# Three small tiles move to the constants pool, and TensorE's operand tiles start at byte 480 of 512

## The chip, the cores and the metric

The kernel runs on one core of one Trainium2 chip. The metric is device time in microseconds (us), as the median of timed runs of the whole program. One execution was also recorded by the hardware profiler; all traces below are such recordings.

## What is computed

One layer of a streaming encoder: 512 positions of width 1,024, everything in float32. Cut to what carries the time:

```python
mod = silu(c) @ w_ada + b_ada                       # 6 vectors of 1,024
xn  = rmsnorm(h, norm1_g) * (1 + sc1) + sh1
p   = xn @ w_in                                     # 512 x 1,024 by 1,024 x 8,200
q,k = silu(causal_dwconv(p[q|k columns]))
y_a = gmlp(p[u], p[v])                              # 128 x 128 mixing per channel group
y_b = mlstm(q, k, p[mv], p[o], p[i], p[f])          # 4 heads of 256, causal
h   = h + g1 * ((sigmoid(p[ga]) * y_a + sigmoid(p[gb]) * y_b) @ w_out)
xn  = rmsnorm(h, norm2_g) * (1 + sc2) + sh2
h   = h + g2 * (relu(xn @ w_ff1) ** 2 @ w_ff2)      # FFN width 4,096
out = rmsnorm(h, final_g)
```

## The kernel before

**Matmuls.** Nearly all the time goes to large matmuls. Each float32 operand is split into a rounded part (`h`) and the rest (`l`), both of TensorE's rounded float32 type, and a product is three matmuls into the same PSUM bank, `mm3` at lines 107 to 109: high by high, high by low, low by high. A matmul takes a stationary operand of 128 columns (`lhsT`, loaded into the array by a weight load of its own) and a moving operand of 512 or 256 columns (`rhs`). In the names of the profile, `out<-moving,stationary`.

**Stages**, in order of time:

1. The start: `x` is transposed, the modulation vectors are summed, and 6 banks of q and k are made in 8 chunks (`mm_w`, line 273): moving `xh`/`xl`, stationary `wh_s`/`wl_s`; 18 matmuls of 512 columns in a chunk.
2. The rest of `w_in`. Twelve "token-major" blocks (`block_tm`: o0, mv0, mv1, gb0, o1, gb1, v0, v1, u0, u1, ga0, ga1) have the weights as moving operand (512 columns) and a 128-column slice of `xh`/`xl` as stationary one; a block is 96 matmuls. Three "feature-major" blocks (`block_fm`: k1, q1 with 96 matmuls, k2 with 48) have it the other way round. Between them stand the scores and the attention products of the mLSTM, and the mixing of the gMLP.
3. The output projection `wo`: moving weights, stationary slices of `mhl`; 192 matmuls of 512 columns.
4. FF1: the first 512 columns (`f10b`, 192 matmuls of 256 columns), then 7 blocks of 7 products (`P`, Strassen-like, 24 matmuls of 256 columns each, 1,176 in all): moving `x2h`, `x2l`, `S..hl`, stationary `wh_B`, `wh_T` and their low parts.
5. FF2 (`ob`): 32 pieces of `w_ff2` of 128 rows, each 24 matmuls of 512 columns, with the weights moving and slices of `hsh`/`hsl` stationary. The first two pieces take their stationary operand from `sc` (`hs` in the names); the last four (`LAST`) have buffers of their own for the weights (`lwh`, `lwl` in `hsp`) and are run token block by token block, with the final norm behind each.

**Feeding.** The DMA queue brings a raw piece into `raws`, ScalarE rounds it (`act.copy`), VectorE subtracts (`dve.tensor_sub`), and the pair lies in `wpool`, three deep, prefetched two ahead (`Stream`). The order of the instructions on an engine is that of the program as built; nothing is decided at run time.

**Where tiles lie.** A pool is a stretch of bytes, the same on all 128 partitions. Pools of the left side are laid one behind the other from the bottom up, those with `side="right"` from the top down, and in a pool each tile starts at the next multiple of 32 bytes. So a small tile shifts every left tile behind it. In `before`, `const` ends at byte 18,816 (36 x 512 + 384), and `raws` and `wpool` follow there. `xpool` holds `yb` (16,384 bytes) and `hs` (64 bytes), which puts `xnp` at byte 448 of 512; `ffp` begins with `ss2` and `rs2` (32 bytes each with their padding), which puts its ring `hT` at byte 0 of 512. Slices of 128, 256, 512 or 1,024 elements step by whole multiples of 512 bytes, so every slice of a tile has its tile's offset. Only `vh` and `vl` (rows of 258 elements) vary.

| tiles | operand of | start, byte of 512 |
|---|---|---|
| `raw_*` (raws) | DMA target | 384 |
| `wh_*`, `wl_*` (wpool) | moving or stationary weights | 384 |
| `xh`, `xl` (xnp) | stationary or moving activations | 448 |
| `q..h`, `k..h` and low parts (attn) | scores | 448 |
| `wo3h` to `wo7l`, `f10..h`, `f10..l`, `h`, two of the eight `x2` pairs (ring `hT`) | wo, f10b | 0 |
| `sc`, `T` (ffp) | first two FF2 pieces | 0 |
| `mhl`, `S..hl` (mhp, right) | wo, P | 480 |
| the other `x2h`, `x2l` (x2p, right) | P, f10b | 480 |
| `hsh`, `hsl`, and `wh_f`, `wl_f` of the last four pieces (hsp, right) | FF2 | 480 |
| `wh_s`, `wl_s` of k at the start (stp, right) | start | 480 |
| `wgs` (right), `ones_r` | gates, row sums | 384, 256 |

Of the kernel before, what the change touches and what calls it, by code (L numbers as in the profile page):

```python
# [8 lines left out]
F32 = mybir.dt.float32  # L9
# [7 lines left out]
P = 128  # L17
# [3 lines left out]
TB = T // P  # L21
H = 4
# [18 lines left out]
V_GI = 144  # L41
V_GF = 145
NV = 146


@with_exitstack
def block_kernel(ctx, tc, vecs_d, rows_d, ws_d, x_d, w_ada, w_in, w_out, w_ff1, w_ff2, out_d):
# [3 lines left out]
    const = ctx.enter_context(tc.tile_pool(name="const", bufs=1))  # L51
# [6 lines left out]

    vecs = const.tile([P, NV], F32, name="vecs")
    ident = const.tile([P, P], F32, name="ident")  # L60
# [10 lines left out]
    def rsq(o, i):  # L71
        pool.tensor_scalar(out=o, in0=i, scalar1=EPS, scalar2=None, op0=ALU.add)
        pool.tensor_tensor(out=o, in0=o, in1=mhalf[:, 0:o.shape[-1]], op=ALU.pow)

    a2 = const.tile([P, KT], F32, name="a2")
    b2 = const.tile([P, KT], F32, name="b2")

# [32 lines left out]

    xpool = ctx.enter_context(tc.tile_pool(name="xpool", bufs=1))
    yb = xpool.tile([P, TB, D], F32, name="yb")
    hs = xpool.tile([P, TB, H], F32, name="hs")

    win = ExitStack()
    xnp = win.enter_context(tc.tile_pool(name="xnp", bufs=1))
# [525 lines left out]
    def ada_acc(base, nm):  # L642
        acc = pp.tile([P, D], F32, tag="acc", name="acc" + nm, bufs=2)

        def piece(k):
            raw = pp.tile([P, D], F32, tag="araw", name=f"ar{nm}{k}", bufs=3)
            sp.dma_start(out=raw, in_=w_ada[k * P:(k + 1) * P, base:base + D])
            if k == 0:
                dve.tensor_scalar(out=acc, in0=raw, scalar1=c_act[:, 0:1], scalar2=None, op0=ALU.mult)
            else:  # L650
                dve.scalar_tensor_tensor(out=acc, in0=raw, scalar=c_act[:, k:k + 1], in1=acc,  # L651
                                         op0=ALU.mult, op1=ALU.add)

        bg.extend([(lambda k=k: piece(k)) for k in range(KT)])
        return acc
# [109 lines left out]
    fp = ff.enter_context(tc.tile_pool(name="ffp", bufs=1))  # L765
    xr = yb
    for t in range(TB):
        sp.dma_start(out=xr[:, t, :], in_=x_d[t * P:(t + 1) * P, :])
    ss2 = fp.tile([P, TB], F32, name="ss2")
    rs2 = fp.tile([P, TB], F32, name="rs2")  # L770
    acc_g2 = ada_acc(5 * D, "g2")

    def pair_banks(nm, pr):
# [373 lines left out]
```

## Time and profile before

| | us |
|---|---|
| median of 3 timed runs | 836.16 |
| their range | 835.72 to 840.86 |
| span of the profiled execution, first to last instruction | 834.4 |
| median less span (what lies around it) | 1.8 |
| TensorE (PE) busy | 822.7 (99%) |
| VectorE (DVE), ScalarE (ACT) busy | 553.4 (66%), 359.5 (43%) |
| DMA, share of 16 engines | 39.6% |

The profile's page gives the busy time of each engine and, in 40 slices of the span, its busy share in tenths. Matmuls are pipelined: the recorded duration of one (389 to 400 ns for 512 columns) is longer than the time from its start to the next one's start. So the rate is read from starts. The view of one tile's instructions gives, for a group, the count, the least, median and greatest duration, and the first and the last start. Where the three lines of `mm3` run in turn, three steps lie between two starts of one line. The view by windows gives the number of matmuls in a stretch of time.

### The profile page before, as it was taken

The numbers are of one execution on the slowest core, as the hardware profiler recorded it, in microseconds if no ns is written. First come the engines' busy times: TensorE is split into PE (matmuls) and PEld (weight loads), VectorE is DVE, ScalarE is ACT, GpSimd is POOL, SyncE is SP. The second block draws the span as 40 slices with busy tenths as digits, with TensorE's granted clock in tenths as the row PEclk, the third lists the DMA queues.
The fourth block names the chain that finished last, engine by engine and source line by source line (L and its number), as shares of the span: only waits on it lengthen the run. The fifth ranks groups of instructions, "written<-read, shape, count | busy, mean of one in ns | idle before, by whom it ended". The sixth has DMA issues, their size and how long they took to land.

```text
span 834.4 us, 11373 instructions
## 1 busy us (share of the span) xinstructions
PE 822.7 (99%) x4427; PEld 700.2 (84%) x4427; DVE 553.4 (66%) x857; ACT 359.5 (43%) x540; POOL 42.2 (5%) x60
## 2 busy tenths in 40 slices
PE   8999999999999999999999999999999999999996
PEld 6887888887888888888888899999999888888885
DVE  5979657584733377888566689888888434443546
ACT  5557456274333233222444456666666221221314
POOL 2003020130100000100000000000000000000000
PEclk9999999999999999999999999999999999999998
DMA  9973331143033398676344231333321422222302
GB/s 274 269 239 107 105 97 26 43 135 101 3 98 101 114 340 290 211 266 218 106 179 144 84 122 49 105 108 114 106 77 65 138 101 101 78 99 101 111 15 102
DMA packets 66822, 107.28 MB, mean 129 GB/s; under 512 B 5328, under 2 KB 38224, under 8 KB 66768
## 3 DMA queue, kind: packets, MB, share of 16 engines
q1 hardware_dynamic: 66768, 106.56, 39.6%
q8 instruction: 35, 0.57, 0.3%
q14 instruction: 19, 0.16, 0.1%
HBM read 104.44 MB, written 2.10 MB: 128 GB/s over the span
## 4 chain that ended last, share of the span: by engine, by line
PE 94%; ACT 1%; DMA 1%; issue 1%; DVE 1%; POOL 0%; SPq 0%; POOLq 0%; DVEq 0%
PE ob L108 7%; PE ob L109 7%; PE ob L107 7%; PE P L107 6%; PE P L108 6%; PE P L109 6%; PE qk L273 4%; PE wo L107 1%; PE wo L108 1%; PE wo L109 1%; PE cp L232 1%; PE k1b L107 1%; PE u1b L107 1%; PE mv1b L109 1%; PE gb0b L108 1%
## 5 line engine op out<-in xcount | busy, mean ns | idle before, releaser
L107 PE MATMUL ob<-wh_f,hsh 128*128 128x512 f32 x240 | 94.9, 395 | 0.0
L108 PE MATMUL ob<-wl_f,hsh 128*128 128x512 f32 x240 | 94.9, 395 | 0.0
L109 PE MATMUL ob<-wh_f,hsl 128*128 128x512 f32 x240 | 94.9, 395 | 0.0
L85 ACT CAST wh_f<-raw_f 128x1024 fp32r<-128x1024 f32 x28 | 29.5, 1053 | 115.2 <-PE ob L109 112.1
L86 DVE TENSOR_TENSOR wl_f<-raw_f,wh_f 128x1024 fp32r<-128x1024 f32 x28 | 34.3, 1225 | 58.2 <-ACT wh_f L85 57.1
L107 PEld LDWEIGHTS ob<-wh_f,hsh 128*128 128x128 f32 x240 | 45.2, 188 | 10.8
L108 PEld LDWEIGHTS ob<-wl_f,hsh 128*128 128x128 f32 x240 | 45.2, 188 | 10.8
L109 PEld LDWEIGHTS ob<-wh_f,hsl 128*128 128x128 f32 x240 | 45.2, 188 | 10.8
L908 ACT CAST wh_T<-T 128x1024 fp32r<-128x1024 f32 x21 | 22.0, 1049 | 24.3 <-PE P L108 23.4
L107 PE MATMUL P<-x2h,wh_B 128*128 128x256 f32 x112 | 31.7, 283 | 0.0
L108 PE MATMUL P<-x2l,wh_B 128*128 128x256 f32 x112 | 31.6, 282 | 0.0
L109 PE MATMUL P<-x2h,wl_B 128*128 128x256 f32 x112 | 31.4, 280 | 0.0
L908 ACT CAST wh_B<-B 128x1024 fp32r<-128x1024 f32 x21 | 22.1, 1051 | 18.1 <-PE P L108 16.7
L1027 DVE CAST hsh<-h 128x512 fp32r<-128x512 f32 x30 | 12.7, 426 | 25.6 <-PE ob L108 25.6
L909 DVE TENSOR_TENSOR wl_T<-T,wh_T 128x1024 fp32r<-128x1024 f32 x21 | 25.7, 1225 | 2.9 <-ACT wh_T L908 2.9
L909 DVE TENSOR_TENSOR wl_B<-B,wh_B 128x1024 fp32r<-128x1024 f32 x21 | 25.6, 1221 | 0.5 <-ACT wh_B L908 0.5
L86 DVE TENSOR_TENSOR wl_gb<-raw_gb,wh_gb 128x1024 fp32r<-128x1024 f32 x8 | 9.8, 1224 | 20.7 <-ACT wh_gb L85 20.7
L1028 DVE TENSOR_TENSOR hsl<-h,hsh 128x512 fp32r<-128x512 f32 x30 | 20.7, 691 | 3.0 <-DVE hsh L1027 0.5
L651 DVE SCALAR_TENSOR_TENSOR accg<-arg,c_act,accg 128x1024 f32<-128x1024 f32 x14 | 17.9, 1282 | 5.2 <-DMA arg<-in_w_ada 5.0
L109 PEld LDWEIGHTS P<-x2h,wl_B 128*128 128x128 f32 x112 | 21.3, 190 | 0.0
L108 PEld LDWEIGHTS P<-x2l,wh_B 128*128 128x128 f32 x112 | 21.0, 188 | 0.0
L107 PEld LDWEIGHTS P<-x2h,wh_B 128*128 128x128 f32 x112 | 20.9, 187 | 0.0
(544 smaller groups left out, 2492.3 us busy)
## 6 DMA issues: line engine op xcount, KB each, us to landing
raw_f<-in_w_ff SPq DMA_DIRECT2D x36, 512.0 KB, 3.3
B<-in_w_ff SPq DMA_DIRECT2D x28, 512.0 KB, 3.8
ar<-in_w_ada SPq DMA_DIRECT2D x64, 128.0 KB, 3.4
arg<-in_w_ada SPq DMA_DIRECT2D x16, 512.0 KB, 5.6
raw_o<-in_w_in SPq DMA_DIRECT2D x8, 512.0 KB, 3.7
raw_mv<-in_w_in SPq DMA_DIRECT2D x8, 512.0 KB, 3.5
raw_gb<-in_w_in SPq DMA_DIRECT2D x8, 512.0 KB, 3.6
raw_v<-in_w_in SPq DMA_DIRECT2D x8, 512.0 KB, 3.5
```

The lines of the kernel that those rows point to most:

```text
L85: act.copy(out=wh, in_=raw)
L86: dve.tensor_sub(out=wl, in0=raw, in1=wh.bitcast(F32))
L107: pe.matmul(out, lhsT=ah, rhs=bh, start=start, stop=False)
L108: pe.matmul(out, lhsT=ah, rhs=bl, start=False, stop=False)
L109: pe.matmul(out, lhsT=al, rhs=bh, start=False, stop=stop)
L232: pe.matmul(cps[c][:, o:o + 1], lhsT=tile_[:, vi, f * P:(f + 1) * P], rhs=rhs, start=first and q == 0, stop=last and q == len(todo) - 1)
L273: pe.matmul(bk, lhsT=wx[:, kk, f * P:(f + 1) * P], rhs=xx[k], start=k == 0 and ps_ == 0, stop=k == KT - 1 and ps_ == 2)
L651: dve.scalar_tensor_tensor(out=acc, in0=raw, scalar=c_act[:, k:k + 1], in1=acc, op0=ALU.mult, op1=ALU.add)
L908: act.copy(out=wh, in_=src)
L909: dve.tensor_sub(out=wl, in0=src, in1=wh.bitcast(F32))
L1027: dve.tensor_copy(out=h_, in_=src)
L1028: dve.tensor_sub(out=l_, in0=src, in1=h_.bitcast(F32))
```

## The change

`hs`, `ss2` and `rs2` become tiles of the constants pool, and an unused tile of 480 bytes follows them there. `const` grows by 64 + 32 + 32 + 480 = 608 bytes and ends at byte 19,424 (37 x 512 + 480). `xpool` then holds `yb` alone, and `ffp` begins with its ring.

```diff
@@ -41,6 +41,7 @@
 NV = 146
+ROW_PAD = 480
@@ -72,6 +73,10 @@
+    hs = const.tile([P, TB, H], F32, name="hs")
+    ss2 = const.tile([P, TB], F32, name="ss2")
+    rs2 = const.tile([P, TB], F32, name="rs2")
+    const.tile([P, ROW_PAD // 4], F32, name="row_pad")
     a2 = const.tile([P, KT], F32, name="a2")
     b2 = const.tile([P, KT], F32, name="b2")
@@ -110,7 +115,6 @@
     yb = xpool.tile([P, TB, D], F32, name="yb")
-    hs = xpool.tile([P, TB, H], F32, name="hs")
@@ -766,8 +770,6 @@
         sp.dma_start(out=xr[:, t, :], in_=x_d[t * P:(t + 1) * P, :])
-    ss2 = fp.tile([P, TB], F32, name="ss2")
-    rs2 = fp.tile([P, TB], F32, name="rs2")
     acc_g2 = ada_acc(5 * D, "g2")
```

All the tiles of the table above then start at byte 480, but for `wgs` and `ones_r`, which stay. `vh`, `vl` and `ph` of the attention move from 160, 224 and 288 to 192, 256 and 320; their distances change little. Pools of the right side do not move.

No engine's instructions change in kind, number or order. Only two waits differ, both on GpSimd (POOL), because `ss2` and `rs2` no longer take bytes that other tiles used before. In the order of GpSimd before, from the first of the second norm's four pairs to the end:

```order
L72 TENSOR_SCALAR rs_3767<-ss_3766 128x1 [waits DMAHW0_49,PE_49,DMAHW1_49,Activation_49,Pool_49]
L73 TENSOR_TENSOR rs_3767<-rs_3767,mhalf 128x1 [waits Pool_49]
L72 TENSOR_SCALAR rs_3767<-ss_3766 128x1 [waits Activation_49]
...
L73 TENSOR_TENSOR rs_3767<-rs_3767,mhalf 128x1 [waits Pool_49]
L1090 TENSOR_TENSOR rs_7227<-rs_7227,mhalf 128x1 [waits DVE_49] x4
```

The same place in the changed kernel:

```order
L73 TENSOR_SCALAR rs_83<-ss_82 128x1 [waits Activation_49]
L74 TENSOR_TENSOR rs_83<-rs_83,mhalf 128x1 [waits Pool_49]
L73 TENSOR_SCALAR rs_83<-ss_82 128x1 [waits Activation_49]
...
L1092 TENSOR_TENSOR rs_7228<-rs_7228,mhalf 128x1 [waits DMAHW0_49,DMAHW1_49,DVE_49,PE_49]
L1092 TENSOR_TENSOR rs_7228<-rs_7228,mhalf 128x1 [waits DVE_49] x3
```

The first pair of the second norm (`rs2`) waits for ScalarE alone now; the first of the last norm (`rs3`), whose bytes now overlap older tiles, waits for two DMA queues and TensorE as well.

## The prediction

> **What bounds the kernel now.** The page first: busy times, TensorE's row of slices and its clock, and the chain that ended last.
>
> ```profile
> PE 822.7 (99%) x4427; PEld 700.2 (84%) x4427; DVE 553.4 (66%) x857; ACT 359.5 (43%) x540; POOL 42.2 (5%) x60
> PE   8999999999999999999999999999999999999996
> PEclk9999999999999999999999999999999999999998
> PE 94%; ACT 1%; DMA 1%; issue 1%; DVE 1%; POOL 0%; SPq 0%; POOLq 0%; DVEq 0%
> ```
>
> TensorE is busy in every slice at full clock and is 94% of the chain. The view of waits, for TensorE alone, says how little it stands still:
>
> ```profile
> PE xt L312 <- POOL epsc L298: 2.5, 1, 2.5
> PE xt L306 <- DVE xt L324: 1.6, 2, 1.3
> PE k1b L107 <- ACT wh_k L85: 0.2, 1, 0.2
> ```
>
> These are 4.3 us of 834.4, and 4.1 of them lie in the first 11 us. No faster transfer or split can help; the end moves only with the step of the matmuls, the time from one start to the next. A busy share doesn't show that step, so I read it from first and last starts, by stage. FF2's loop and its last four pieces, in the view of the tile `ob` (count, duration in ns least/median/greatest, first and last start):
>
> ```profile
> L107 PE MATMUL ob<-wh_f,hsh x200: 392/397/400, 659.6 to 799.5; 128*128 128x512 f32 x100
> L107 PE MATMUL ob<-wh_f,hsh x31: 389/389/389, 805.8 to 826.2; 128*128 128x512 f32 x31
> ```
>
> In the loop 199 x 3 steps take 139.9 us: 234.3 ns each. In the last pieces 30 x 3 steps take 20.4 us: 226.7 ns, and all 31 durations are the same to the nanosecond. It is the same matmul with the same kind of stationary operand (`hsh`, byte 480); the moving operand lies at 384 in the loop and at 480 in the last pieces. The other stages of 512 columns:
>
> ```profile
> L107 PE MATMUL mv1b<-wh_mv,xh x32: 394/394/394, 179.6 to 201.3; 128*128 128x512 f32 x32
> L107 PE MATMUL u0b<-wh_u,xh x32: 393/396/398, 331.4 to 353.1; 128*128 128x512 f32 x32
> L107 PE MATMUL k2b<-xh,wh_k x16: 392/392/392, 168.6 to 178.9; 128*128 128x512 f32 x16
> L108 PE MATMUL k2b<-xl,wh_k x16: 394/394/394, 168.8 to 179.1; 128*128 128x512 f32 x16
> L109 PE MATMUL k2b<-xh,wl_k x16: 388/388/389, 169.1 to 179.3; 128*128 128x512 f32 x16
> L107 PE MATMUL ob<-wh_f,hs x16: 390/393/404, 647.8 to 658.2; 128*128 128x512 f32 x16
> L107 PE MATMUL wo<-wh_wo,mhl x24: 391/398/476, 431.3 to 474.0; 128*128 128x512 f32 x24
> L107 PE MATMUL wo<-wo4h,mhl x8: 393/395/397, 444.0 to 476.8; 128*128 128x512 f32 x8
> L273 PE MATMUL qk<-xh,wh_s x42: 388/392/503, 21.7 to 56.9; 128*128 128x512 f32 x42
> ```
>
> Token-major blocks (moving 384, stationary 448): 21.7 us / 93 = 233.3 ns, in `mv1b` and in `u0b`. Feature-major (448, 384): 10.3 / 45 = 228.9. First FF2 pieces (384, 0): 10.4 / 45 = 231.1. `wo` is broken by other work, so I go by its median durations: a duration is 162 to 163 above its step (397 and 234.3; 389 and 226.7), so 398 and 395 (moving 384 and 0, stationary 480) make about 235 and 232.5. The start's 392 makes 229.5. So each pair of offsets has a step of its own, and the last pieces have the shortest. Their durations repeat without any spread, as if two periodic things stood at a fixed distance; that is my reading of it.
>
> **Does it need equal offsets, or the quiet end of the program?** FF1's first block answers. In its second half the first two pairs have both operands at byte 0, the others 480 against 0, with the same work around them:
>
> ```profile
> L107 PE MATMUL f10b<-x2h,f100h x8: 280/283/283, 495.1 to 497.6; 128*128 128x256 f32 x8
> L108 PE MATMUL f10b<-x2l,f100h x8: 283/283/283, 495.2 to 497.7; 128*128 128x256 f32 x8
> L108 PE MATMUL f10b<-x2l,f104h x8: 277/280/285, 501.1 to 503.6; 128*128 128x256 f32 x8
> 495.18 0.28 PE L108 MATMUL f10b<-x2l,f100h 128*128 128x256 f32 x1
> 497.70 0.28 PE L108 MATMUL f10b<-x2l,f100h 128*128 128x256 f32 x1
> 500.98 0.28 PE L107 MATMUL f10b<-x2h,f104h 128*128 128x256 f32 x1
> 506.30 0.28 PE L107 MATMUL f10b<-x2h,f106h 128*128 128x256 f32 x1
> ```
>
> Equal: all at 283 after the first, 21 steps in 2.52 us, 120.0 ns. Unequal: spread from 277 to 285, 45 steps in 5.32 us, 118.2 ns. So the fixed step comes with equal offsets in the middle of the program too, and at 256 columns it is no gain. The products, unequal now (480, 384), stand at 120.0: the view by windows, for the tile `P` (start:end, length, busy time and count of TensorE):
>
> ```profile
> 540.00:600.00 60.00, 60.00 (x502) 60.00 (x501) 13.94 (x21) 1.74 (x3) 1.00 0.35 106
> ```
>
> A matmul lasts some 0.28 us, so two or three of the 502 began before the window; 500 in 60.00 us is 120.0 ns.
>
> **The change part by part.** All pairs become 480 and 480. I take 226.7 ns for 512 columns and 120.0 ns for 256:
>
> - token-major, 12 x 96 = 1,152 matmuls: (233.3 - 226.7) = 6.6 ns each, 7.6 us
> - FF2, 28 pieces of 24 in the loop: 26 x 24 = 624 x 7.6 = 4.7 us, and the first two, 48 x 4.4 = 0.2 us; the last 96 gain nothing
> - `wo`, 72 x 8.3 + 120 x 5.8 = 1.3 us
> - feature-major, 240 x 2.2 = 0.5 us
> - the start, 144 x 2.8 = 0.4 us
>
> Together 14.7 us over 2,400 matmuls. Against it: `f10b`, 144 of its 192 go from 118.2 to 120.0, 0.3 us; and finding the fixed step again after a break, where the row of `f100h` shows one odd matmul (280 before 283). At 30 breaks, an estimate, of 10 ns (three odd matmuls of about 3 ns) that is 0.3 us. The 1,176 products: nothing, from 120.0 to 120.0. Their bounds: 116.1 (the gain of 512 columns in proportion, 226.7 / 234.3) and 123 (a duration of 286, the longest of the low rows, less 163): 4.6 us less to 3.5 us more. I take the row of `f100h`, the same shape with equal offsets. Scores, attention products, transposes, gates and row sums: too few, or their distance stays; nothing.
>
> What the moved bytes do elsewhere. Splits and casts on the two kinds of offset that are there already:
>
> ```profile
> L85 ACT CAST wh_f<-raw_f 128x1024 fp32r<-128x1024 f32 x28 | 29.5, 1053 | 115.2 <-PE ob L109 112.1 <-PE P L108 3.1
> L1051 ACT CAST wh_f<-raw_f 128x1024 fp32r<-128x1024 f32 x4 | 4.2, 1046 | 4.5 <-DMA raw_f<-in_w_ff 4.5
> L86 DVE TENSOR_TENSOR wl_f<-raw_f,wh_f 128x1024 fp32r<-128x1024 f32 x28 | 34.3, 1225 | 58.2 <-ACT wh_f L85 57.1
> L1052 DVE TENSOR_TENSOR wl_f<-raw_f,wh_f 128x1024 fp32r<-128x1024 f32 x4 | 4.9, 1220 | 2.0 <-ACT wh_f L1051 2.0
> B<-in_w_ff SPq DMA_DIRECT2D x28, 512.0 KB, 3.8
> raw_f<-in_w_ff SPq DMA_DIRECT2D x36, 512.0 KB, 3.3
> ```
>
> Writing to 480 (the rows of four) takes what writing to 384 takes, 1,046 and 1,053 ns, 1,220 and 1,225 ns. Half of the 28 transfers `B` land at 480, half at 384, and their common 3.8 us is far within the lead: ScalarE waits 112 us in the FF2 loop for TensorE to free a buffer. A piece will take 24 x 226.7 = 5.4 us there instead of 5.6; the split needs 1.05 and 1.23 us of it. So the cover stays. Where it is thin I bound the loss: the 0.2 us wait of `k1b` can grow by what `o0b` gains, 96 x 6.6 = 0.6 us; `wo`'s 1.3 and the start's 0.4 can be lost if splits and loads don't come earlier. Padding costs no instruction. GpSimd's changed waits: `rs2` loses waits for things long past, and the first `rs3` gains them behind a wait for VectorE that lasts to the end anyway; only four small powers and the last output are queued behind it, and TensorE's work is over. Nothing either way.
>
> The sum: 14.7 - 0.3 - 0.3 = 14.1 us, span 834.4 - 14.1 = 820.3, and with the 1.8 us that lie around the span 822.1, some 1.7% below the median of 836.16.
>
> [...]
>
> **The rivals.**
>
> [...] 7%.
>
> *The products gain too*, at 116.1: 4.6 us more, 817.5. Against it, the row of `f100h`. 6%.
>
> *The gain is given back at thin places.* Up to 0.6 + 1.3 + 0.4 us from above, and a slower return to the fixed step: six steps lost at each of 30 breaks, 30 x 6 x 6.6 ns = 1.2 us. Together 3.5: 825.6. For it, the waits of `k1b`, and the fact that the scores, below, never settled. 9%.
>
> *Slower: equal offsets collide.* The scores have both operands at 448 now. Their second head, durations by group:
>
> ```profile
> L108 PE MATMUL sc<-q2l,k2h 128*128 128x512 f32 x1 | 0.4, 402 | 0.0
> L109 PE MATMUL sc<-q2h,k2l 128*128 128x512 f32 x1 | 0.4, 396 | 0.0
> L107 PE MATMUL sc<-q3h,k3h 128*128 128x512 f32 x1 | 0.4, 397 | 0.0
> L109 PE MATMUL sc<-q3h,k3l 128*128 128x512 f32 x1 | 0.4, 387 | 0.0
> ```
>
> Equal, yet not settled within six matmuls, and one at 402, a step of 239. If the long runs settled there, the 1,152 would lose 5.7 ns, the 672 of the loop about 4.9, `wo` about 5.6, the other 384 about 9.9: 6.6 + 3.3 + 1.1 + 3.8 = 14.8 us, 851. It decides from a step of 232.9 on, the mean of the 2,400 now. Against it, the last pieces settled at 389 within three matmuls. 3%.
>
> That the tiles don't lie where the change says is excluded: the sizes in front of them add up to 480. The remaining 75% is the forecast.
>
> **How the numbers follow.** The forecast itself spreads from 820 to 824 (steps known to 0.5 ns over 2,400 matmuls). The range takes in the gain of the products below and the thin places above, with half of the distance to no effect: 817 to 828. Outside lie no effect, slower, and a little else, about 12%. A measurement of this kernel tells 1% (8.4 us) from no change: faster by that is below 827.8, which holds for the forecast, the products and the thin places, 0.89; within 1% for no effect and a half gain, 0.08; slower 0.03.
>
> **What would show it.** In the changed profile `ob`'s and the token-major rows should read 389/389/389, with 93 steps of a block in 21.1 us instead of 21.7; `k2b`'s three lines should become alike; `P` should keep 500 matmuls in 60 us, at 283 without spread. TensorE's waits should stay under 6 us. I am wrong if the token-major rows keep a spread around 394, if `P` leaves 120, or if new waits of TensorE for `wh_` tiles appear.

## The result, and the profile after

The changed kernel took 824.24 us (median of 4 runs, 822.58 to 824.85), the kernel before 836.45 us (median of 4, 835.72 to 840.86). The ratio is 0.9837, with a 95% interval of 0.9805 to 0.987. A second measurement of the same two kernels (below) gave 0.9837 again, 0.9818 to 0.9856. The profiled execution of the changed kernel took 822.58 us, the lowest of its four runs; its span is 820.8 us, against 834.4 before.

The page of the changed kernel: busy times, TensorE's slices and its clock, and the chain that ended last.

```profile
PE 809.9 (99%) x4427; PEld 702.0 (86%) x4427; DVE 553.2 (67%) x857; ACT 359.5 (44%) x540; POOL 42.1 (5%) x60
PE   8999999999999999999999999999999999999996
PEclk9999999999999999999999999999999999999999
PE 97%; DVE 1%; issue 1%; ACT 1%; DMA 0%; POOL 0%; POOLq 0%
```

TensorE's busy time fell by 12.8 us, VectorE's and ScalarE's stayed. TensorE is still busy in every slice and carries more of the chain, 97% instead of 94%. The view of its waits:

```profile
PE xt L316 <- POOL epsc L302: 2.5, 1, 2.5
PE xt L310 <- DVE xt L328: 0.7, 1, 0.7
PE k1b L112 <- ACT wh_k L90: 0.2, 1, 0.2
```

The same three waits, 3.4 us instead of 4.3, and no new one; the whole difference lies in `xt`, in the start. The matmuls by tile (count, duration in ns least/median/greatest, first and last start; the lines of `mm3` are 112 to 114 now): FF2 with its first two pieces in the second row, two token-major blocks, the feature-major one, `wo`, and the products.

```profile
L112 PE MATMUL ob<-wh_f,hsh x240: 388/389/390, 650.1 to 812.6; 128*128 128x512 f32 x120
L112 PE MATMUL ob<-wh_f,hs x16: 389/389/397, 639.2 to 649.4; 128*128 128x512 f32 x16
L112 PE MATMUL mv1b<-wh_mv,xh x32: 388/389/390, 178.3 to 199.4; 128*128 128x512 f32 x32
L112 PE MATMUL u0b<-wh_u,xh x32: 389/389/390, 326.4 to 347.5; 128*128 128x512 f32 x32
L112 PE MATMUL k2b<-xh,wh_k x16: 389/389/390, 167.5 to 177.7; 128*128 128x512 f32 x16
L113 PE MATMUL k2b<-xl,wh_k x16: 389/389/390, 167.7 to 177.9; 128*128 128x512 f32 x16
L114 PE MATMUL k2b<-xh,wl_k x16: 389/389/390, 167.9 to 178.1; 128*128 128x512 f32 x16
L112 PE MATMUL wo<-wh_wo,mhl x24: 389/390/476, 423.9 to 465.7; 128*128 128x512 f32 x24
L112 PE MATMUL P<-x2h,wh_B x112: 282/283/284, 498.1 to 627.3; 128*128 128x256 f32 x112
```

What stood at 394 and 397 stands at 389, with 1 ns of jitter; 93 steps of a token-major block take 21.1 us, as `u0b` shows; the three lines of `k2b` are alike; `P` stays at 283. Over all uninterrupted pairs of starts in `ob` the mean step is 226.7 ns.

Where the 13.6 us between the two spans came from, by the first start of each stage's first tile in the two traces (us; the forecast is the term of the sum):

| from, to | before | after | gain | forecast |
|---|---|---|---|---|
| span's start to `o0b` | 58.01 | 58.39 | -0.38 | 0.4 |
| `o0b` to `wo` (12 token-major and 3 feature-major blocks, attention, mixing) | 373.28 | 365.55 | 7.7 | 8.1 |
| `wo` to `f10b` | 50.36 | 49.24 | 1.1 | 1.3 |
| `f10b` to `P` | 24.99 | 24.91 | 0.1 | -0.3 |
| `P` to `ob` | 141.11 | 141.12 | 0.0 | 0 |
| `ob` to the span's end | 186.59 | 181.59 | 5.0 | 4.9 |

### The profile page after: what moved, and what is told of

Its sections match the earlier page's. It is cut to its first block, busy times and chain, and to the rows that moved or that the text cites. A ratio compares the mean times of both kernels' runs of the same rounds, so it can differ in the third digit from the quotient of the medians.

```text
span 820.8 us, 11373 instructions
## 1 busy us (share of the span) xinstructions
PE 809.9 (99%) x4427; PEld 702.0 (86%) x4427; DVE 553.2 (67%) x857; ACT 359.5 (44%) x540; POOL 42.1 (5%) x60
## 4 chain that ended last, share of the span: by engine, by line
PE 97%; DVE 1%; issue 1%; ACT 1%; DMA 0%; POOL 0%; POOLq 0%
PE ob L112 7%; PE ob L114 7%; PE ob L113 7%; PE P L114 6%; PE P L113 6%; PE P L112 6%; PE qk L277 4%; PE wo L112 2%; PE wo L114 2%; PE wo L113 2%; PE f10b L113 1%; PE f10b L112 1%; PE f10b L114 1%; PE k1b L112 1%; PE cp L236 1%; PE o0b L114 1%
## 5 line engine op out<-in xcount | busy, mean ns | idle before, releaser
L113 PEld LDWEIGHTS P<-x2l,wh_B 128*128 128x128 f32 x112 | 21.5, 192 | 0.0
L114 PEld LDWEIGHTS P<-x2h,wl_B 128*128 128x128 f32 x112 | 21.5, 192 | 0.0
L112 PEld LDWEIGHTS P<-x2h,wh_B 128*128 128x128 f32 x112 | 21.5, 192 | 0.0
L655 DVE SCALAR_TENSOR_TENSOR accg<-arg,c_act,accg 128x1024 f32<-128x1024 f32 x14 | 17.9, 1282 | 4.4 <-DMA arg<-in_w_ada 4.2
```

The costliest lines, as they stand in the source:

```text
L112: pe.matmul(out, lhsT=ah, rhs=bh, start=start, stop=False)
L113: pe.matmul(out, lhsT=ah, rhs=bl, start=False, stop=False)
L114: pe.matmul(out, lhsT=al, rhs=bh, start=False, stop=stop)
```

## The experiments

Two readings of the first traces are at odds with the forecast's: that byte 480 itself is a good place, and that the offsets don't matter and something else in the last pieces (their buffers, the quiet end) shortens the step. A third question is whether equal offsets are the best ones.

**One series per pair of offsets.** A program of its own that runs nothing but matmuls of the same types, 96 for each pair; the layer's computation is left out entirely. `COUNT` is 96, and a line of `CASES` has the name, the columns, and the byte of the moving and of the stationary operand.

```python
for nm, n, mo, so in CASES:
    banks = [psum.tile([P, 512], F32, tag="ps", name=nm) for _ in range(2)]
    for i in range(COUNT):
        m0 = mo // 4 + 512 * (i % 3)
        s0 = so // 4 + 128 * (i % 8)
        pe.matmul(banks[(i // 3) % 2][:, 0:n], lhsT=sta[:, s0:s0 + P], rhs=mov[:, m0:m0 + n], start=True, stop=True)
```

> A program of its own that leaves the whole layer out (its output is a copy of x): 34 series of 96 matmuls in the rounded float32 type, each with another start byte (of 512) of the moving and of the stationary operand, nothing else running. Theory 'distance': the step depends only on moving start less stationary start; equal starts give 226.7 ns at 512 columns wherever they lie (series eqA at 480, eqB at 0, eqC at 256, eqD at 100), unequal ones 229 to 235 (qA, moving 448 and stationary 384: 229; qB, the other way round: 233), and 120.0 at 256 columns for equal starts (hA), 118.2 for moving 480 and stationary 0 (hI). Rival 'byte 480': only eqA reaches 226.7, eqB to eqD stay above 231. Rival 'offsets do not matter': all series of a width alike. Rival 'collision': equal series show steps of 239.

The rows of nine series: both operands at 0, at 256 and at 100; the moving operand 64 above, 96 below and 64 below the stationary one, 512 columns; then 256 columns with both at 0, 64 above and 64 below.

```profile
L48 PE MATMUL eqB<-mov,sta x96: 387/389/398, 33.4 to 55.0; 128*128 128x512 f32 x96
L48 PE MATMUL eqC<-mov,sta x96: 389/389/389, 55.2 to 76.7; 128*128 128x512 f32 x96
L48 PE MATMUL eqD<-mov,sta x96: 392/400/403, 77.0 to 99.6; 128*128 128x512 f32 x96
L48 PE MATMUL pD<-mov,sta x96: 388/392/394, 167.3 to 189.0; 128*128 128x512 f32 x96
L48 PE MATMUL pK<-mov,sta x96: 390/397/400, 322.6 to 344.8; 128*128 128x512 f32 x96
L48 PE MATMUL pL<-mov,sta x96: 391/394/394, 345.1 to 367.2; 128*128 128x512 f32 x96
L48 PE MATMUL hA<-mov,sta x96: 280/283/283, 478.8 to 490.2; 128*128 128x256 f32 x96
L48 PE MATMUL hD<-mov,sta x96: 276/276/279, 513.3 to 524.1; 128*128 128x256 f32 x96
L48 PE MATMUL hH<-mov,sta x96: 276/276/276, 558.5 to 569.3; 128*128 128x256 f32 x96
```

95 steps of `eqC` take 21.5 us, some 226 ns each; those of `pK` 22.2 us, some 234 ns. From the starts to the nanosecond, the mean step behind the 30th matmul of a series, beside the step of the same pair in the kernel before:

| columns; moving, stationary | distance | in `before` | series |
|---|---|---|---|
| 512; 480, 480 | 0 | 226.7 (last FF2 pieces) | 226.66 |
| 512; 384, 448 | -64 | 233.3 (token-major) | 233.34 |
| 512; 448, 384 | +64 | 228.9 (feature-major) | 228.94 |
| 512; 384, 480 | -96 | 234.3 (FF2 loop) | 234.29 (at 416, 0) |
| 512; 384, 0 | -128 | 231.1 (first FF2 pieces) | 232.35 |
| 256; 0, 0 | 0 | 120.0 (`f10b`) | 120.00 |
| 256; 480, 0 | -32 | 118.2 (`f10b`) | 118.29 |
| 256; 480, 384 | +96 | 120.0 (`P`) | 119.91 (at 96, 0) |

A program in which VectorE, ScalarE and GpSimd are busy for 0.00 us from 20 to 640 us, with a DMA share of 0.00, gives the kernel's steps again, seven of eight within 0.2 ns. The eighth, 231.1, was read from starts rounded to 0.1 us; to the nanosecond that stage's mean step in the kernel is 232.5, and its steps run 228, 230, 233, 241, 232, 231 like those of the series. So the offsets alone are enough for these steps, and the rival "offsets don't matter" fails. At 512 columns no distance of the 15 tried beat 0 (distance 256 equals it, the others give 228.9 to 238.5). Equal offsets at 0, 256 or 480 all give 226.7, but at byte 100 the equal pair takes 237.6, which the expectation above had at 226.7. And at 256 columns equal offsets are not the best: 113.3 ns at +64 and -64 against 120.0.

**Without the padding, and the padding alone.** The first kernel is the changed one without the padding tile: the three tiles are moved, and the left-hand operands start at byte 0 instead of 480. The second is the kernel before with 96 bytes of padding and nothing moved, which puts `wpool` at 480, `xh` at 32 and the ring at 96.

```diff
# first: the changed kernel
-    const.tile([P, ROW_PAD // 4], F32, name="row_pad")
# second: the kernel before
+    const.tile([P, 24], F32, name="row_pad")
     a2 = const.tile([P, KT], F32, name="a2")
```

> The three tiles move, the padding is left out: all left tiles start at byte 0, the right ones stay at 480. Theory 'distance': token-major and feature-major blocks gain as in the changed kernel (7.6 + 0.5 us), the start 0.3; FF2's loop and wo become 0 against 480, some 232.5 ns (1.1 + 0.2 + 0.2 us); the products become 480 against 0, 118.2 ns (2.1 us): 11.7 us after 0.3 for breaks, span about 822.7, time about 824.5, and P's step is below 120. Rival 'byte 480': the blocks at 0 and 0 gain nothing, time 832 to 836.

> The three tiles stay where they were, 96 bytes of padding put the weights at byte 480, xh and xl at 32, the ring at 96. Theory 'distance': FF2's loop and the first three pieces of wo become equal and gain 4.7 + 0.6 us; the token-major blocks (480 against 32) keep the distance of 448 against 0 they had and stay at 233.3, the feature-major ones at 229: span about 829, time about 831. Rival 'a moving operand at byte 480 is enough': the token-major blocks gain too, 7.6 us more: about 823.5.

Without the padding: 827.87 us, ratio 0.9885 (0.9867 to 0.9904), span 826.5. The tiles of its token-major block (0, 0) and its FF2 loop (0, 480), and then the window of the products (480, 0):

```profile
L111 PE MATMUL mv1b<-wh_mv,xh x32: 389/389/389, 180.3 to 201.3; 128*128 128x512 f32 x32
L111 PE MATMUL ob<-wh_f,hsh x240: 389/394/397, 651.7 to 818.4; 128*128 128x512 f32 x120
```

```profile
540.00:600.00 60.00, 60.00 (x509) 60.00 (x508) 14.02 (x21) 1.73 (x3) 1.00 0.36 107
```

The padding alone: 832.85 us, ratio 0.9939 (0.9919 to 0.996), span 829.1. Its token-major block (480, 32) and its FF2 loop (480, 480):

```profile
L108 PE MATMUL mv1b<-wh_mv,xh x32: 394/394/394, 179.8 to 201.5; 128*128 128x512 f32 x32
L108 PE MATMUL ob<-wh_f,hsh x240: 389/389/389, 658.4 to 820.9; 128*128 128x512 f32 x120
```

FF2 gains 4.8 us and `wo` 0.5 here, as expected. Each kernel has the short step of 512 columns just where its two operands are level, and the long one elsewhere. Byte 480 for the weights alone gives the token-major blocks nothing (394), byte 0 for both gives them all of it (389). The first kernel's span came out 3.8 us above what was expected. By stages against the changed kernel: FF2 and `wo` take 4.11 and 1.10 us more, the products 1.96 us less (507 in 60 us are 118.3 ns each), `f10b` 0.54 more: together 3.8 us, where the terms of the expectation and of the forecast make 2.3. In FF2's loop (0 against 480, +32) the step is 233.3 ns as at +32 in the series, not the 232.5 of the expectation. The other 2.0 us lie ahead of `q1b`, 0.5 in the start and 1.5 in one place, shown next.

**The changed kernel once more.** The median gain of the first runs, 12.2 us, is below the sum's 14.1 and the spans' 13.6.

> The changed kernel once more, beside the kernel before on one chip, so that the size of the gain is known better than from the first runs (12.2 us between medians; 13.6 us between the two profiled spans; 14.1 us by the sum). If the sum's 14.1 us are right and the first median was only drawn from few runs, the ratio is 0.9833 (13.5 to 14.1 us). If part of the gain is given back (rival 'thin places', 10.6 us), the ratio is 0.987. I expect 0.983 to 0.985, and steps of 226.7 ns (512 columns) and 120.0 ns (P) as before.

825.10 us against 837.91 (9 runs of the kernel before), 12.8 us, ratio 0.9837. The profiled execution has a span of 823.3, 2.5 us more than the first one's. All stages behind the attention agree with the first trace to 0.02 us but for `f10b`, 0.3 us longer. The differences are 0.7 us in the start and 1.5 us in the scores. The view by windows there (start:end, length, busy time and count of PE, PEld, DVE, ACT and POOL, granted clock, DMA share, GB/s), first of the first trace, then of this one:

```profile
125.00:137.00 12.00, 12.00 (x65) 9.11 (x65) 8.81 (x17) 7.30 (x17) 1.28 (x1) 1.00 0.17 45
```

```profile
125.00:137.00 12.00, 12.00 (x58) 9.22 (x58) 7.29 (x13) 7.50 (x17) 0.98 (x1) 0.86 0.17 45
```

The granted clock is 0.86 instead of 1.00 there, and TensorE gets through 58 matmuls instead of 65. The kernel without the padding has the same 0.86 in that window, and so has the one with the products at a distance of 64 (below); the kernel before, the one with the padding alone and the one with all at byte 0 have 1.00. From the scores' first start to `q1b`'s it takes 17.8 to 17.9 us in the three traces with the dip and 16.3 in the four without. So an execution can lose 1.5 us to the clock there, and the two traces that the table of stages compares did not.

In the start the clock dips once in both traces of the changed kernel, to 0.79 from 12 to 20 us in the first and from 20 to 28 us in this one; whether the 0.7 us come from that is not shown. The changed kernel's other three runs of the first series took 1.6 to 2.3 us longer than the profiled one. Their mean granted clocks are 0.994, 0.996 and 0.995; the trace without the dip has 0.996, this one 0.994. The first of them may have met the dip; the one that took longest (0.996) shows no sign of it, and what its 2.3 us are made of stays open.

**All at byte 0.** Every pool of both sides is shifted so that the operands of the large matmuls start at 0.

```diff
-ROW_PAD = 480
+ROW_PAD = 512
     const = ctx.enter_context(tc.tile_pool(name="const", bufs=1))
+    rpad = ctx.enter_context(tc.tile_pool(name="rpad", bufs=1, side="right"))
+    rpad.tile([P, 120], F32, name="right_pad")
```

> Padding of 512 bytes and 480 bytes on the right side put all the operand tiles that the change puts at 480 at byte 0. Theory 'distance': as the changed kernel, 822 to 825, all steps of 512 columns at 226.7. Rival 'byte 480': no gain, 834 or more.

823.35 us, ratio 0.9838 (0.9814 to 0.9862), span 820.8: the changed kernel's time.

```profile
L114 PE MATMUL mv1b<-wh_mv,xh x32: 389/389/389, 177.7 to 198.7; 128*128 128x512 f32 x32
L114 PE MATMUL ob<-wh_f,hsh x240: 389/389/389, 650.2 to 812.7; 128*128 128x512 f32 x120
```

Byte 480 is no better than byte 0. In this kernel it is the distance of the two operands that counts: both at 0 and both at 480 give the median of 389 ns, 0 against 480 gave 394 above.

**The products at a distance of 64.** The first series promised 6.7 ns for each of the 1,176 products. A tile of 64 bytes above the right-hand pools of the products' activations moves these to 416; the weights stay at 480.

```diff
     mhs = ExitStack()
+    mvpad = mhs.enter_context(tc.tile_pool(name="mvpad", bufs=1, side="right"))
+    mvpad.tile([P, 16], F32, name="mv_pad")
     mp = mhs.enter_context(tc.tile_pool(name="mhp", bufs=1, side="right"))
```

> The changed kernel with one more tile of 64 bytes above the right-hand pools of the products' activations: mhl, S..hl and six of the eight x2 pairs start at 416 instead of 480; everything else stays at 480. Theory 'distance of the two operands, and the best one depends on the columns': the 1,176 products (moving 416, stationary 480, distance -64) step 113.3 ns instead of 120.0, 7.8 us less; 144 of f10b go from 119.8 to 113.3, 0.9 us less; wo (moving 480, stationary 416, distance +64) goes from 226.7 to 228.85 ns, 0.4 us more. Sum 8.3 us less than the changed kernel: about 815 us, ratio to before 0.973. Rival 'equal offsets are always best' (the reading in the prediction): P leaves 120.0 for a spread like f10b's 118.2 or worse, 2 us less at most. Rival 'VectorE takes over': VectorE is busy 34.3 of 40 us in the products; by the shorter step that is 34.3 of 37.8; if it became the bound, TensorE's waits for wl_B and wl_T would appear there and half of the 7.8 us would be lost.

816.19 us (814.62 to 817.03), ratio to the kernel before 0.9736 (0.9722 to 0.9749); 8.9 us below the changed kernel on the same chip, 8.3 expected. A group of products, their window, and the largest new row of the view of waits:

```profile
L112 PE MATMUL P<-x2h,wh_B x112: 276/276/276, 500.4 to 622.5; 128*128 128x256 f32 x112
```

```profile
540.00:600.00 60.00, 60.00 (x532) 60.00 (x531) 14.34 (x22) 2.16 (x4) 1.00 0.36 108
```

```profile
PE u1b L112 <- ACT ug L736: 1.0, 1, 1.0
```

All 1,176 steps are 113 or 114 ns; from the first product to FF2 it is 133.28 us instead of 141.12, the 7.84 us of the sum. Between the two profiled spans it is 8.1 us, and not all of that is the products: the start is 1.3 us shorter, `f10b` 0.6 us (0.9 expected), `wo` takes 0.3 us more (0.4 expected), and `u0b` to `u1b` 1.3 us more. No wait appeared in the products, so VectorE didn't take over. The wait in `u1b` comes from further back: ahead of the `ug` activations ScalarE waits 7.4 us for VectorE's sum `accsc`, and VectorE has waited 4.6 us in all for the transfers `arsc` that this sum reads. In the two traces of the changed kernel these two waits are 1.2 and 0.5 us, and 3.5 and 3.2 us. The sum's pool lies behind the new tile and moves with it, so whether the tile has a part in the wait is not shown. The reading "equal offsets are always best" is wrong at 256 columns: 113 or 114 ns here, 120.0 with level operands.

**Finer distances, and the same distances again.** The program of series twice more, with 72 matmuls each.

> The program of series again, alone on the chip (the whole layer is left out): 72 matmuls each, stationary operand at byte 0, the moving one at distances not tried so far, for 512, 256, 384 and 128 columns. If the step depends on the distance modulo 256 bytes in steps of 32 or 64, +160 is like -96 (234.3) and +208 like -48, and +224 like -32 (233.3). [...] I expect none below 226.67 at 512 columns and 113.33 at 256 columns, and multiples of 64 better than what lies between.

No step below 226.66 at 512 columns and none below 113.32 at 256 appeared. But a distance of +240 gave 226.66 where its neighbours +224 and +248 gave 233.38 and 237.74, and -16 had given 233.34. At 256 columns +112 gave 113.34, -112 118.72, and +192 113.34 as well. At 384 columns the six distances gave 175.0 to 176.7, -64 176.68. So two distances 256 apart can be alike (0 and +256 both 226.7 at 512 columns, +192 and -64 both 113.3 at 256) or not (+240 and -16), and the last run asked whether the distance alone decides.

> The program of series a third time (the whole layer is left out), 72 matmuls each. First part: distances that gave odd values are repeated behind other predecessors and at byte 480. If the distance alone sets the step, every repetition gives the same: 512 columns 0: 226.7, -16: 233.3, +240: 226.7, -96: 234.3, -64: 233.3, +64: 228.9; 256 columns 0: 120.0, +112: 113.3, -112: 118.7, +64 and -64: 113.3; 384 columns +64 and 0: 173.3, -64: 176.7. Rival: the offsets at the start of a series decide between several steps that repeat themselves, so that -16 can settle at 226.7 and +240 at 233.3; then at least one of the repetitions differs by 2 ns or more. Second part: the stationary operand always the same 128 columns, or the moving one always the same slice. If only the distance of the two streams within 512 bytes counts, nothing changes (226.7, 234.3, 233.3, 228.9 and 120.0, 113.3); if the rotation of the slices counts, the steps differ.

It doesn't. In this run, 512 columns at +240 twice and at 0 between; then 256 columns at +64, at -64, and at 416 against 480, the pair of the products above:

```profile
L80 PE MATMUL aB<-mov,sta x72: 396/396/396, 44.9 to 61.5; 128*128 128x512 f32 x72
L80 PE MATMUL aC<-mov,sta x72: 389/389/389, 61.7 to 77.8; 128*128 128x512 f32 x72
L80 PE MATMUL aF<-mov,sta x72: 392/398/403, 111.7 to 128.5; 128*128 128x512 f32 x72
L80 PE MATMUL aG<-mov,sta x72: 389/389/397, 128.7 to 144.9; 128*128 128x512 f32 x72
L80 PE MATMUL bE<-mov,sta x72: 279/279/280, 278.8 to 287.1; 128*128 128x256 f32 x72
L80 PE MATMUL bG<-mov,sta x72: 276/276/286, 295.8 to 303.9; 128*128 128x256 f32 x72
L80 PE MATMUL bH<-mov,sta x72: 280/281/281, 304.0 to 312.3; 128*128 128x256 f32 x72
```

At +240 the series settled at 233.34 and at 236.72, after 226.66 in the run before; with the stationary operand at 480 it was 233.32. At 256 columns and +64 it was 117.79 (113.32 before), at -64 113.34, and at 416 against 480, also -64, 117.79. At 384 columns -64 gave 174.66 and 173.32. So the same pair settled on several mean steps. The three series of +240 with the stationary operand at 0 stood behind different ones, +224 (226.66), -16 (233.34) and -96 (236.72); what decides between the steps is not shown. Not every pair moved. Level operands at byte 0, 256 or 480 gave 226.7 at 512 columns in all ten series of the three programs, and level ones at 0 or 480 gave 120.0 at 256. At 256 columns +112 came back at 113.34 twice. Nor did -96 at 512 columns (234.3), -64 (233.3 to 233.4) and +64 (228.8 to 229.0) leave their values. Holding the stationary operand, or the moving one, on the same slice throughout changed nothing: 226.7, 234.3, 233.3 and 229.0 again. What in the chip makes these steps stays open.

## Why the prediction was right

The mechanism held in this kernel: the step of a 512-column matmul follows from where the two operands lie to one another, level operands at byte 480 settle at 226.7 ns, and TensorE was the bound and stayed it. Two readings that went with it did not hold. "Each pair of offsets has a step of its own" is true of the pairs of this kernel at 512 columns, but +240 had three. And durations without spread are not the mark of level operands: `mv1b` in the kernel before, at 394/394/394 with a step of 233.3 ns, had none either, and level operands at byte 100 spread from 392 to 403. What is level can be told from the place of the tiles and the length of the step, not from the spread. Point by point:

- **The steps that were read from `before`** are the series' steps, in seven of eight pairs to 0.2 ns; the eighth, the first FF2 pieces, was misread by 1.4 ns, less than 0.1 us over its 48 matmuls. Reading the step from first and last starts of a stage, by pairs of offsets, was enough to see the difference between the pairs in one trace.
- **Token-major and feature-major**, 8.1 us: 7.7 us measured, with the attention and the mixing between them. The six token-major blocks from `gb0b` to `u0b`, with nothing between, gave 3.81 us from the first start to the last, and 576 x 6.6 ns is 3.80.
- **FF2**, 4.9 us: 5.0. **`wo`**, 1.3 us: 1.1.
- **The products**, 0: 141.11 and 141.12 us. That `f100h`'s row sets their step, rather than the gain of 512 columns in proportion, was right. That the old pair (+96, 119.9 ns in its series, with a spread) comes to the same as the level one is a coincidence, which the prediction read off the trace. The rival "products gain too" failed here; that they have 113.3 in them at another distance was seen by neither.
- **`f10b`**, 0.3 us lost: 0.1 us gained in the first trace. Its stage lasts 24.91, 25.25 and 25.77 us in three traces that all have level operands there (all at byte 0, and the changed kernel twice), so the term is smaller than the stage's own spread.
- **The start**, 0.4 us gained: 0.4 us lost. This is the term with the wrong sign. The stage lasts 57.7 to 59.1 us in the seven profiled executions of the layer; a gain of 0.4 us can't be seen in it. Its short runs of matmuls also settled only in part: the mean step of `qk` without its breaks is about 228.8 ns after the change, not 226.7.
- **Thirty breaks of 10 ns**: right in sum as far as can be seen, though not in the size of one. `aG` above took five odd steps, 29 ns in all, to settle, `aC` none.
- **The thin places** held: the wait of `k1b` stayed at 0.2 us, and no wait for a `wh_` tile was added.
- **Sum and time.** 14.1 us forecast, 13.6 between the spans. The time forecast, 822.1, lies 0.5 us from the profiled execution, 822.58; the median, 824.24, lies 2 us higher, still within the range. The forecast took the profiled execution of the kernel before (836.16) for the usual one, and in later series that kernel's median was 837.8 and 837.9. A second trace of the changed kernel shows 1.5 us of such a difference as a clock of 0.86 in the scores; for the rest no cause is shown.

"Slower: equal offsets collide" rested on six scores at 448 that didn't settle. The series settle at 226.7 with level operands at bytes 0, 256 and 480, `eqB` only after seven odd steps: 230, 225, 230, 236, 229, 232 and 231 ns. The first head's scores in the kernel before go through 225, 230, 236, 229 and 232, the second to the sixth of these: by that they were on the way there, and six matmuls were too few to arrive. That level operands at 448 would have settled at 226.7 is an estimate from this likeness.

From pair to pair of offsets the step of 512 columns went from 226.7 to 238.5 ns in the first program of series, where from 20 us on no other engine was busy.

## What to carry to other kernels

Where matmuls follow one another without a pause, read the step from starts, by stage and shape, and set it beside the byte of 512 at which each operand begins; a stage whose durations spread, or stand apart from those of the same shape elsewhere, may have a few per cent in its tile offsets (here 226.7 instead of 234.3 ns, 3.2%), to be had with some bytes of padding. For 512 columns in this type, nothing tried was better than level operands, and at bytes 0, 256 and 480 they settled on the same 226.7 ns each time; for 256 columns a distance of 64 bytes gave 5.6% less than level ones, but can settle at 117.8 instead of 113.3 ns, so it has to be measured in its kernel. One trace gives the steps; a second one of the same kernel shows how much two executions differ for other reasons, here 2.5 us.

## What the runs showed of the hardware

- The same pair of offsets settled on several mean steps (512 columns at +240: 226.66, 233.34, 236.72 ns; 256 columns at +64: 113.32 and 117.79). With level operands at bytes 0, 256 and 480 only one was seen.
- Level operands aren't always the short case: both at byte 100, 237.6 ns; both at 0, 256 or 480, 226.7. Byte 100 is the only other place of level operands in the series, and what sets it apart is not shown. With the stationary operand at 0, the moving one at other bytes gave 226.7 to 238.5 ns.
- At 128 columns the offsets made no difference: 111.6 to 111.7 ns at the six distances tried.
- Ahead of the first series TensorE waits 10 us, and its first step then lasts 590 ns and the next ones 427 until 13.2 us, a little under twice the settled one, while the granted clock of the window reads 1.00:

```profile
L48 PE MATMUL eqA<-mov,sta x96: 387/389/792, 10.0 to 33.2; 128*128 128x512 f32 x96
```

```profile
0.00:15.00 15.00, 4.95 (x15) 3.97 (x16) 1.23 (x1) 3.18 (x2) 0.20 (x4) 1.00 0.78 307
```

The view reads 1.00 for the first 10 us too, in which TensorE ran nothing: it also shows 1.00 where the trace has no record of the clock, and here the first record begins at 13.2 us. So at the start of this program the 1.00 is no proof that the matmuls ran at their later pace; the steps of 427 ns against 226.7 show that they did not.
